# Delta-net layers in another column order, with one block substitution on VectorE

## The chip, the cores and the metric

The kernel runs on one core of one Trainium2 chip. The metric is the device time of one execution in microseconds. The kernel before takes 2232.32 us, the median of 3 runs (2231.94 to 2232.71). In the text PE is TensorE, DVE is VectorE, ACT is ScalarE, POOL is GpSimd and SP is SyncE, the engine that issues most transfers.

## The reference

Four layers work on 256 tokens of 1024 features. Each is a feed-forward half step, a token mixer and another feed-forward half step. The mixers of layers 0 and 3 are gated delta nets, that of layer 1 is a short convolution, that of layer 2 a sparse attention. Only the delta nets are touched by the change:

```python
def gdn_mixer(h, w_in, conv_w, A_log, dt_bias, out_norm, w_out):
    proj = h @ w_in                                   # queries, keys, values, gate: 4 x 1024; a, b: 2 x 8
    qkv, gate, a, b = jnp.split(proj, [...], axis=-1)
    qkv = jax.nn.silu(causal_depthwise_conv(qkv, conv_w))      # width 4
    q, k = l2norm(q), l2norm(k)                                # 8 heads of 128
    beta = jax.nn.sigmoid(b)
    g = -jnp.exp(A_log) * jax.nn.softplus(a + dt_bias)
    o = gated_delta_rule_chunked(q, k, v, g, beta)
    o = rmsnorm(o, out_norm) * jax.nn.silu(gate)
    return o @ w_out

# within a chunk: A = strictly lower part of (beta k) k^T times the decay;
# u and w are solutions with the unit triangular matrix (I + A); then a scan over the chunks:
v_new = u_c - w_c @ state
o = (q * decay) @ state + attn @ v_new
state = state * g_last + k_dec^T @ v_new
```

## The kernel before

All activations lie with features on partitions and the 256 tokens in the free dimension. Every product with weights is made three times in float32r, from two parts of the weights and two of the activations (`mm3`, L297 to L299). `Weights` streams the weights through 4 raw buffers. SP issues the loads (L90, L92) in the order of use, and a load waits until its buffer is free. ACT writes the high part (`hi`, L108, 128x1024) and DVE the rest (`lo`, L116); in the delta net, nine of the rests go to POOL instead (`tiles(..., nc.gpsimd, ...)`).

In the delta net (`gdn`) a `Dense` object emits the products one row tile at a time ("step": 6 matmuls of 256 columns), and after each step it lets every pending follow-up ("tail") emit its next piece (`pump`). So one order, fixed when the program is built, decides what stands behind what in the queue of each engine. `meet(condition)` emits steps until a tail has reached a state. When no products are left, steps emit only tails.

The columns come as 8 pairs (query, key) of a head, then 8 pairs (value, gate). `head_in` scales the product (L728), convolves (L695 on ACT, three L700 on DVE for each column tile) and applies silu through tanh (L703, L705). `head_mid` makes the transposes (L745), the decays (L748, L764 and the exponentials on ACT) and the products of keys with keys and queries (L753, L768). After 4 heads `lanes` starts for that half. It scales the matrices (L806), writes their 32x32 diagonal blocks to DRAM (L811, tile `db`), reads them back so that a partition holds a part of one block (L823, M in tile `gi`), inverts all 32 blocks by 31 steps of a multiplication and an addition on POOL (L830, L832, tile `g_inv`), writes the inverses to DRAM (L836, `di`) and reads them into their places on the diagonal (L840). `merges` then joins blocks of 32 to 64 and 128 (it begins with the transposes L852, then L870, L883, L887), `scan` runs the recurrence over two blocks of 128 tokens (L905 to L925) and `finish` norms, gates and splits the output (L937 to L956). This is done for heads 0 to 3 and then for heads 4 to 7; `wait(n)` lets a tail skip n steps. The output product (`add_rows_steps`) fills the second half's chain. The next norm begins with its sums of squares (L280).

The transfers of `lanes` go through SP's queue, between the loads of weights. The source of L823 is written out by hand; its leading dimension has 4 copies with stride 0:

```python
bass.AP(tensor=flat.tensor, offset=flat.offset, ap=[[0, 4], [1024, 32], [1, 1024]])
```

Of the kernel before, what the change touches and what calls it, by code (L numbers as in the profile page):

```python
# [28 lines left out]
class Weights:  # L29
    """Streams weights from DRAM in the order of use and splits them into two float32r parts whose  # L30
    sum is the float32 weight. A piece is what a run of products takes, in two halves."""
# [68 lines left out]
    def hi(self):  # L100
        """Writes the next half piece's part that float32r holds, once there is room for it."""
# [9 lines left out]
    def lo(self, engine=None):  # L111
        """Writes what remains of it."""
# [7 lines left out]
    def ahead(self, i, engine=None):  # L120
        """Every piece up to i has been split, as far as there is room."""
# [17 lines left out]
    def part(self, i, k):  # L139
        """Row tile k of piece i in its two parts."""  # L140
# [5 lines left out]
def kernel(ctx, tc, plan, a, out):  # L146
# [21 lines left out]
    def add_pairs(w):  # L168
        """Columns of the left half and the same of the right half."""
# [22 lines left out]
    def add_wide(w, c):  # L192
        """512 columns, each piece a half of the rows."""
# [40 lines left out]
    def busy(times):  # L234
        """The tensor engine's clock is at its full rate only after a few microseconds of products."""
# [12 lines left out]
    class Normed:  # L248
        """x * norm weight in two float32r parts, and the sums of squares on their way to the
        reciprocal root, which is applied behind the products."""  # L250
# [25 lines left out]
    def norm_sums(n):  # L276
        """The reciprocal roots, tokens on partitions."""
# [7 lines left out]
    def norm_rows(n):  # L285
        """The same for all partitions: a token to a column."""
# [17 lines left out]
    def rest(steps):  # L304
        """What a stream of steps returns at its end."""
# [6 lines left out]
    def output(k):  # L312
        """Two feature tiles of the result, tokens on partitions."""
# [9 lines left out]
    def add_rows_steps(pieces, inputs, ktiles, scale, next_col, engine=None):  # L323
        """x += scale * (inputs @ weights), the weights' rows in `pieces`; the next norm's start."""
# [44 lines left out]
    def first_cols(j, acc, ks, n):  # L369
        """The first products: those with the smaller parts of the weights behind the others."""  # L370
# [10 lines left out]
    def two_cols(j, acc, ks, n):  # L381
        """Two column tiles, which the piece keeps side by side in each row tile."""
# [15 lines left out]
    def two_first(pieces, n):  # L398
        """The first two pieces behind a norm."""
# [109 lines left out]
    def gdn_masks():  # L509
# [11 lines left out]
        def before(n, name):  # L521
            """The column's block of 2**n follows the row's in the same block of 2**(n + 1)."""
# [9 lines left out]
        G.half = const.tile([128, 8], F32, name="half")  # L532
        nc.vector.memset(G.half, 0.5)
        G.m1, p = before(5, "gm1")
        i32 = t2("i32", (8, 32), I32)
        nc.gpsimd.iota(i32, pattern=[[-4, 8], [1, 32]], base=0, channel_multiplier=0)
        G.eye32 = const.tile([128, 8, 32], F32, name="eye32")
        nc.vector.tensor_copy(G.eye32, i32)
        nc.vector.tensor_scalar(G.eye32, G.eye32, p[:, :1], None, op0=OP.is_equal)
        G.m2, _ = before(6, "gm2")  # L540
# [9 lines left out]
    def gdn_loads(g, i):  # L550
        """Everything small that the mixer needs, loaded during what comes before it."""
# [8 lines left out]
        on = small("onorm", (1,))  # L560
        nc.gpsimd.dma_start(on, a["gdn_out_norm"][i].rearrange("(p o) -> p o", o=1))
# [11 lines left out]
        g.on = small("onhalf", (1,))  # L573
        nc.vector.tensor_scalar(g.on, on, 0.5, None, op0=OP.mult)

    def gdn_decays(g, n):
        """The token gates: step sizes and cumulated log decays, tokens on partitions."""
# [25 lines left out]
        # log(1 + e) = 2 artanh(e / (2 + e)), the argument at most 1/3  # L603
# [23 lines left out]
    def converted(k, engine=None, other=None):  # L627
        """The conversions that go with a step of eight."""
# [7 lines left out]
    def tiles(j, n, engine=None, other=None):  # L636
        """Two column tiles, features on partitions."""
# [10 lines left out]
    class Dense:  # L648
        """Products by row tiles, and what is done with each, as a stream which is emitted in steps
        between those of a chain."""  # L650
# [28 lines left out]
        def products(self):  # L679
            """The rest of the products; tails may remain."""  # L680
# [11 lines left out]
    def conv_silu(t, taps, tiles, o):  # L692
# [3 lines left out]
        yield from wait(2)  # L696
# [5 lines left out]
        yield from wait(4)  # L702
        nc.scalar.activation(t, o, AF.Tanh, scale=0.5)  # L703
        yield from wait(2)
        nc.vector.scalar_tensor_tensor(o, t, 1.0, o, op0=OP.add, op1=OP.mult)  # L705
# [4 lines left out]
    def gdn(pieces, n, next_col, g):  # L710
        qk, vg, outs = pieces
        ss = small("ss", (2, 4, 2, 2))
        cq = small("gcq", (2, 4, 2))
        QK, H = {}, []
        for half in range(2):
            # by half of the heads: products of keys, queries in decays; two inverses; values, recurrence
            h = Gdn()
            h.ready, h.values = False, 0
            h.ga = b8(F32, "ga", (4, 2, 2, 128))
            k = b8(F32, "gk", (4, 4, 128))  # L720
            h.kE, h.kd, h.qd, h.g0 = (k[:, q] for q in range(4))
# [10 lines left out]
        def head_in(h, acc):  # L732
            t = yield from scaled(acc)
            o = l2("g_qk")
            yield from conv_silu(t, g.taps, (h, 8 + h), o)
            yield from wait(5)
            QK[h] = o

        def head_mid(h):
            x, f = QK[h], H[h // 4]  # L740
            e = h % 4
            pk = mid().rearrange("p (t s c) -> p t s c", t=2, s=2)
            for t in range(2):
                for s in range(2):
                    nc.tensor.transpose(pk[:, t, s], x[:, s, t * 128:(t + 1) * 128], ident)  # L745
            pg = mid()[:, :256].rearrange("p (t c) -> p t c", t=2)
            for t in range(2):
                nc.tensor.matmul(pg[:, t], g.g[:, t, h:h + 1].to_broadcast([128, 128]), G.tri,  # L748
                                 start=t == 0, stop=False, skip_group_check=True)
            pa = mid().rearrange("p (t s c) -> p t s c", t=2, s=2)  # L750
            for t in range(2):
                c = slice(t * 128, (t + 1) * 128)
# [240 lines left out]
        for _ in outputs(0, "mid"):  # L993
            dense.fill(2)
            if H[1].ready:
                next(other, None)
# [613 lines left out]
```

## Time and profile before

| what | value |
|---|---|
| median of 3 runs | 2232.32 us |
| profiled execution, span from first to last instruction | 2231.7 us |
| PE busy | 2149.7 us, 96% |
| DVE busy | 1427.9 us, 64% |
| ACT busy | 1067.2 us, 48% |
| POOL busy | 493.2 us, 22% |
| delta net of layer 0, from 203.4 us to the next norm's sums | 209.7 us, PE busy 184.0 |
| delta net of layer 3, from 1836.0 us to the next norm's sums | 207.5 us, PE busy 181.9 |

The busy shares are averages over stages with different limits, so the table sets the two delta nets apart. The time around the span is 0.6 us.

### The profile page before, as it was taken

How to read it: one execution, taken by the hardware profiler on the slowest of the kernel's cores; microseconds unless marked ns; L12 is line 12 of the kernel's file. 1: busy time of each engine (PE TensorE's matmuls, PEld its weight loads, DVE VectorE, ACT ScalarE, POOL GpSimd, SP SyncE). 2: the span in 40 equal slices, each digit the busy share in tenths (PEclk: the TensorE clock that was granted, in tenths of full speed). 3: DMA queues.
4: the chain of work that ended last, by engine and by line, in shares of the span. 5: the costliest groups of instructions: out<-in, count | busy, mean ns of one | idle time of the engine just before them, and what ended most of it. 6: DMA issues, size and time to landing. Idle time of an engine off the chain costs nothing.

```text
span 2231.7 us, 42671 instructions
## 1 busy us (share of the span) xinstructions
PE 2149.7 (96%) x17615; PEld 2105.6 (94%) x17615; DVE 1427.9 (64%) x2199; ACT 1067.2 (48%) x1830; POOL 493.2 (22%) x619
## 2 busy tenths in 40 slices
PE   8999879999999999999999988899999998979999
PEld 8999879999999999999999877699999998979999
DVE  7755975665566476664765577675566558956653
ACT  5444654544454354543544544454445445625542
POOL 2211473121022020220220233222002103741210
PEclk9999999999999999999999998999999999989999
DMA  7555253555465555655655432155546553524652
GB/s 247 191 190 166 87 135 105 166 189 189 160 199 190 185 174 166 212 189 182 187 190 198 161 123 71 44 188 187 192 150 211 190 170 114 138 86 130 204 196 76
DMA packets 285475, 364.33 MB, mean 163 GB/s; under 512 B 22640, under 2 KB 250096, under 8 KB 285280
## 3 DMA queue, kind: packets, MB, share of 16 engines
q1 hardware_dynamic: 284288, 360.26, 49.6%
q8 instruction: 138, 2.26, 0.4%
q0 software_dynamic: 944, 1.33, 0.3%
q14 instruction: 57, 0.47, 0.1%
q10 hardware_dynamic: 48, 0.02, 0.0%
HBM read 358.94 MB, written 2.10 MB: 162 GB/s over the span
## 4 chain that ended last, share of the span: by engine, by line
PE 82%; DVE 8%; POOL 5%; issue 2%; ACT 2%; DMA 1%; SPq 0%; POOLq 0%; ACTq 0%; DVEq 0%
PE acc L297 16%; PE acc L299 16%; PE acc L298 16%; PE mid L297 9%; PE mid L298 9%; PE mid L299 9%; DVE g_qk L700 2%; POOL g_inv L832 2%; POOL g_inv L830 2%; DMA gi<-db 1%; PE acc L1473 1%; PE mid L1193 1%; DVE wlo L116 1%; PE acc L1111 0%; PE acc L1113 0%
## 5 line engine op out<-in xcount | busy, mean ns | idle before, releaser
L297 PE MATMUL acc<-xhi,whi 128*128 128x256 f32 x3544 | 1006.6, 284 | 0.0
L299 PE MATMUL acc<-xhi,wlo 128*128 128x256 f32 x3544 | 996.7, 281 | 0.5 <-DVE wlo L116 0.5
L298 PE MATMUL acc<-xlo,whi 128*128 128x256 f32 x3544 | 996.4, 281 | 0.0
L116 DVE TENSOR_TENSOR wlo<-raw,whi 128x1024 fp32r<-128x1024 f32 x634 | 774.1, 1228 | 256.4 <-ACT whi L108 256.3
L108 ACT ACTIVATE whi<-raw 128x1024 fp32r<-128x1024 f32 x668 | 696.6, 1052 | 341.2 <-PE mid L298 279.8
L297 PEld LDWEIGHTS acc<-xhi,whi 128*128 128x128 f32 x3544 | 671.0, 189 | 8.3 <-issue 7.2
L298 PEld LDWEIGHTS acc<-xlo,whi 128*128 128x128 f32 x3544 | 670.8, 189 | 0.7
L299 PEld LDWEIGHTS acc<-xhi,wlo 128*128 128x128 f32 x3544 | 670.3, 189 | 0.7 <-DVE wlo L116 0.7
L297 PE MATMUL mid<-hhi,whi 128*128 128x256 f32 x1408 | 395.0, 281 | 0.0
L299 PE MATMUL mid<-hhi,wlo 128*128 128x256 f32 x1408 | 394.8, 280 | 0.0
L298 PE MATMUL mid<-hlo,whi 128*128 128x256 f32 x1408 | 394.8, 280 | 0.0
L428 POOL TENSOR_TENSOR t_h<-t_gate,rb 128x256 f32<-128x256 f32 x176 | 196.5, 1116 | 743.9 <-ACT t_gate L424 741.0
L298 PEld LDWEIGHTS mid<-hlo,whi 128*128 128x128 f32 x1408 | 265.3, 188 | 0.0
L299 PEld LDWEIGHTS mid<-hhi,wlo 128*128 128x128 f32 x1408 | 265.2, 188 | 0.0
L297 PEld LDWEIGHTS mid<-hhi,whi 128*128 128x128 f32 x1408 | 265.2, 188 | 0.0
L424 ACT ACTIVATE t_gate<-t_gate 128x256 f32<-128x256 f32 x176 | 73.6, 418 | 313.1 <-DVE t_gate L423 313.1
L423 DVE TENSOR_TENSOR t_gate<-acc,rb 128x256 f32<-128x256 f32 x176 | 74.3, 422 | 191.6 <-PE acc L299 191.6
L430 DVE TENSOR_TENSOR t_h<-acc,t_h 128x256 f32<-128x256 f32 x176 | 74.7, 424 | 127.6 <-POOL t_h L428 127.6
L435 ACT ACTIVATE hhi<-t_h 128x256 fp32r<-128x256 f32 x176 | 73.6, 418 | 150.0 <-DVE t_h L430 150.0
L116 POOL TENSOR_TENSOR wlo<-raw,whi 128x1024 fp32r<-128x1024 f32 x34 | 83.3, 2458 | 228.5 <-ACT whi L108 164.1
L283 POOL TENSOR_TENSOR rcol<-rcol,neghalf 128x2 f32<-128x2 f32 x12 | 8.5, 704 | 457.5 <-DVE rcol L282 457.5
L437 DVE TENSOR_TENSOR hlo<-t_h,hhi 128x256 fp32r<-128x256 f32 x176 | 73.7, 419 | 7.7 <-ACT hhi L435 7.7
(430 smaller groups left out, 2059.2 us busy)
## 6 DMA issues: line engine op xcount, KB each, us to landing
raw<-in_ffn_w_gate_up_dram SPq DMA_DIRECT2D x350, 512.0 KB, 4.9
raw<-in_ffn_w_down_dram SPq DMA_DIRECT2D x88, 1024.0 KB, 4.8
raw<-in_gdn_w_in_dram SPq DMA_DIRECT2D x64, 512.0 KB, 5.3
raw<-in_nsa_w_in_dram SPq DMA_DIRECT2D x10, 1024.0 KB, 4.9
raw<-in_gdn_w_out_dram SPq DMA_DIRECT2D x8, 1024.0 KB, 9.2
raw<-in_sc_w_in_dram SPq DMA_DIRECT2D x16, 512.0 KB, 4.5
raw<-in_sc_w_in_dram SPq DMA_DIRECT2D x4, 1024.0 KB, 6.7
raw<-in_sc_w_out_dram SPq DMA_DIRECT2D x4, 1024.0 KB, 5.5
```

The lines of the kernel that those rows point to most:

```text
L108: self.nc.scalar.activation(self.parts[g][0], raw, AF.Copy)
L116: (engine or self.nc.vector).tensor_sub(self.parts[g][1], self.half(g), self.parts[g][0])
L297: nc.tensor.matmul(o, w[0], x[0], start=first, stop=False, skip_group_check=True)
L298: nc.tensor.matmul(o, w[0], x[1], start=False, stop=False, skip_group_check=True)
L299: nc.tensor.matmul(o, w[1], x[0], start=False, stop=last, skip_group_check=True)
L423: nc.vector.tensor_mul(t, acc[:, 0], n.rb)
L424: nc.scalar.activation(s, t, AF.Silu)
L428: nc.gpsimd.tensor_mul(sr, s, n.rb)
L430: nc.vector.tensor_mul(h, acc[:, 1], sr)
L435: nc.scalar.activation(hi, h, AF.Copy)
L437: nc.vector.tensor_sub(lo, h, hi)
L700: nc.vector.scalar_tensor_tensor(o[:, s, j:], t[:, s, :S - j], taps[:, c:c + 1], o[:, s, j:], op0=OP.mult, op1=OP.add)
```

## The change

1. The weights' columns come in another order: keys of heads 0 to 3, values of heads 0 to 3, the same of heads 4 to 7, then the gates, then the queries. A product of keys, values or queries now covers two heads of one kind. All rests of weights (L116) are on DVE.
2. The gates are computed with tokens on partitions by `wide` (matmuls of 512 columns) and go through one silu each on ACT (L876), straight from PSUM. `finish` multiplies by them ahead of the transposes.
3. Values and queries use the silu of ACT (L856, L839). Keys keep the tanh.
4. `lanes` runs once for all 8 heads: 64 blocks of 32x32, a partition holds every second row of one, and the 31 steps are on DVE (L919, L923, L925). Its transfers are issued by ACT.
5. `merges` of both halves run side by side, then the two scans, offset by two stages. The output product starts behind most of them.

The core of the diff (the rest is the follow-ups' rearrangement into `keys_in`, `queries_in`, `values_in`, and comments):

```diff
-            steps.append((add_pairs(w[:, :2 * D]), add_pairs(w[:, 2 * D:4 * D]), add_rows(a["gdn_w_out"][i], D)))
+            kv = [add_cols(w, d + c, 512) for c in (0, 512) for d in (D, 2 * D)]
+            steps.append((kv, [add_wide(w, 3 * D + c) for c in (0, 512)], add_cols(w, 0, D),
+                          add_rows(a["gdn_w_out"][i], D)))
...
+        def gates_in(q, accs):
...
+                nc.scalar.activation(h.gates[t], accs[t].rearrange("p (e c) -> p e c", e=4), AF.Silu,
+                                     scale=n.r[:, t:t + 1])
...
-                nc.sync.dma_start(db[b].rearrange("h e c -> e h c"), h.B[r, :, r])
+                    nc.scalar.dma_start(db[b, 8 * q:8 * q + 8].rearrange("m e c -> e m c"), h.B[r, :, r])
...
-            nc.sync.dma_start(M.rearrange("p x c -> p (x c)"),
-                              bass.AP(tensor=flat.tensor, offset=flat.offset, ap=[[0, 4], [1024, 32], [1, 1024]]))
-            yield from wait(10)
+            nc.scalar.dma_start(M.rearrange("p x c -> p (x c)"),
+                                bass.AP(tensor=flat.tensor, offset=flat.offset, ap=[[0, 2], [1024, 64], [1, 1024]]))
+            yield from wait(LM)
...
             for k in range(31):
-                e, c = k // 4 + 1, 31 - k
+                e, c = k // 2 + 1, 31 - k
...
-                nc.gpsimd.tensor_mul(t, M[:, k:k + 1, k + 1:].to_broadcast([128, e, c]),
+                nc.vector.tensor_mul(t, M[:, k:k + 1, k + 1:].to_broadcast([128, e, c]),
                                      V[:, :e, k:k + 1].to_broadcast([128, e, c]))
-                nc.gpsimd.tensor_add(V[:, :e, k + 1:], V[:, :e, k + 1:], t)
...
+                nc.vector.tensor_add(V[:, :e, k + 1:], V[:, :e, k + 1:], t)
...
-                nc.sync.dma_start(di.rearrange("b h (i r) c -> (b h) r i c", r=4)[:, r], V[32 * r:32 * r + 32])
+                nc.scalar.dma_start(di.rearrange("b m (i r) c -> (b m) r i c", r=2)[:, r], V[64 * r:64 * r + 64])
...
-                nc.sync.dma_start(h.iv[r, :, r], di[b].rearrange("h e c -> e h c"))
+                nc.scalar.dma_start(iv[r, :, r], di[b].rearrange("m e c -> e m c"))
...
-        dense = Dense([(tiles(qk[h], n, nc.gpsimd if h > 0 else None, nc.gpsimd if h < 3 else None), lambda acc, h=h: head_in(h, acc[0])) for h in range(8)]
-                      + [(tiles(vg[m], n), lambda acc, m=m: vg_in(m, acc[0])) for m in range(8)])
+        dense = Dense([(tiles(kv[2 * q + x][e], n), lambda acc, p=2 * q + e, f=f: f(p, acc[0]))
+                       for q in range(2) for x, f in enumerate((keys_in, values_in)) for e in range(2)]
+                      + [(wide(gs[q], n), lambda accs, q=q: gates_in(q, accs)) for q in range(2)]
+                      + [(tiles(qs[p], n), lambda acc, p=p: queries_in(p, acc[0])) for p in range(4)])
...
+        dense.meet(lambda: "inverses" in done)
+        both = [merges(q, "mid") for q in range(2)]
+        for _ in both[0]:
+            next(both[1], None)
+            dense.fill(F1)
```

Where the transfers of the blocks stand. Before, SP's queue in layer 0 holds them between loads of weights:

```order
L90 DMA raw<-in_gdn_w_in_dram 128x4x256 x24
L811 DMA db<-ga 32x8x32 x4
L823 DMA gi<-db 128x1x1024
L90 DMA raw<-in_gdn_w_in_dram 128x4x256 x8
L811 DMA db<-ga 32x8x32 x4
L823 DMA gi<-db 128x1x1024
L92 DMA raw<-in_gdn_w_out_dram 128x2x1024 x2
L836 DMA di<-g_inv 256x1x32 x4
L840 DMA gi<-di 32x8x32 x4
```

After, ACT's queue holds them between its own work (here the second half's blocks, `db`, and the one load of M into `givt`):

```order
L108 ACTIVATE whi<-raw 128x1024 x2
L900 DMA db<-ga 32x8x32 x4
L826 ACTIVATE gk<-gk,ekd 128x128
L827 ACTIVATE gk<-gk,egc 128x128
L826 ACTIVATE gk<-gk,ekd 128x128
L827 ACTIVATE gk<-gk,egc 128x128
L868 ACTIVATE gv<-mid,gsv 128x128 x8
L911 DMA givt<-db 128x1x1024
L856 ACTIVATE g_vc<-g_vc 128x512
```

The load of M moved from SP's queue, where the blocks' writes stand directly ahead of it, into ACT's, where twelve small operations stand between.

Where the substitution stands. Before, POOL's queue in layer 0 has it almost to itself (`gk` is one product of queries and decays):

```order
L832 TENSOR_TENSOR g_inv<-g_inv 128x29
L830 TENSOR_TENSOR g_inv<-gi,g_inv 128x28
L832 TENSOR_TENSOR g_inv<-g_inv 128x28
L830 TENSOR_TENSOR g_inv<-gi,g_inv 128x54
L832 TENSOR_TENSOR g_inv<-g_inv 128x2x27
L762 TENSOR_TENSOR gk<-g_qk,g_dec 128x128
L830 TENSOR_TENSOR g_inv<-gi,g_inv 128x52
```

After, it is in DVE's queue, with the rests of the weights (`wlo`) between its steps:

```order
L116 TENSOR_TENSOR wlo<-raw,whi 128x1024 x4
L919 SCALAR_TENSOR_TENSOR givt<-givt 128x31
L919 SCALAR_TENSOR_TENSOR givt<-givt 128x30
L923 TENSOR_TENSOR givt<-givt 128x58
L925 TENSOR_TENSOR givt<-givt 128x2x29
L923 TENSOR_TENSOR givt<-givt 128x56
L925 TENSOR_TENSOR givt<-givt 128x2x28
```

The substitution moved from POOL to DVE; 4 rests of weights stand ahead of it, and 6 more and one L747 stand between its 60 operations.

## Rows read from the trace of the kernel before

**Rows 1.** The page's first part: busy time, share of the span, instructions.
```profile
span 2231.7 us, 42671 instructions
PE 2149.7 (96%) x17615; PEld 2105.6 (94%) x17615; DVE 1427.9 (64%) x2199; ACT 1067.2 (48%) x1830; POOL 493.2 (22%) x619
```

**Rows 2.** Windows, delta nets: length, busy PE, PEld, DVE, ACT, POOL, clock, DMA.
```profile
203.40:413.10 209.70, 184.04 (x1508) 178.65 (x1506) 158.95 (x261) 112.01 (x285) 93.57 (x156) 0.96 0.38 114
1836.00:2043.50 207.50, 181.86 (x1474) 176.52 (x1474) 155.33 (x253) 108.10 (x276) 93.37 (x156) 0.95 0.38 111
```

**Rows 3.** Windows, stretches of layer 0's delta net.
```profile
203.40:335.20 131.80, 108.74 (x869) 104.96 (x867) 111.66 (x175) 75.44 (x200) 75.65 (x113) 0.95 0.41 116
...
230.00:270.00 40.00, 32.95 (x247) 31.60 (x247) 37.30 (x49) 25.03 (x79) 17.90 (x11) 0.96 0.35 106
...
320.00:335.20 15.20, 2.44 (x22) 2.21 (x20) 5.14 (x8) 2.71 (x4) 12.30 (x39) 0.65 0.12 20
335.20:340.00 4.80, 4.80 (x30) 4.80 (x31) 0.77 (x2) 2.12 (x6) 3.86 (x13) 0.68 1.01 385
340.00:413.10 73.10, 70.50 (x612) 68.89 (x611) 46.51 (x85) 34.45 (x80) 14.06 (x32) 1.00 0.30 94
```

**Rows 4.** Waits of PE, 190 to 420 us: total, times, longest.
```profile
PE mid L852 <- DMA gi<-di: 12.8, 1, 12.8
PE mid L745 <- DVE g_qk L705: 4.1, 2, 3.4
PE mid L764 <- ACT g_dec L756: 4.0, 4, 2.3
```

**Rows 5.** Timeline of SP, POOL and PE: start, length, instruction, idle before.
```profile
274.39 0.65 SPq L823 DMA_DIRECT2D gi<-db  x1
...
284.92 0.39 POOL L830 TENSOR_TENSOR g_inv<-gi,g_inv 128x31 f32<-128x31 f32 x1 [5.84 <-DMA gi<-db]
...
327.35 0.21 POOL L832 TENSOR_TENSOR g_inv<-g_inv 128x8 f32<-128x8 f32 x1
...
327.58 2.60 SPq L836 DMA_DIRECT2D di<-g_inv  x4
...
335.17 1.97 PE L852 MATMUL mid<-ident,gi 128*128 128x128 f32 x8 [12.76 <-DMA gi<-di]
```

**Rows 6.** Windows while L823 alone moves data: length, clock, DMA share, GB/s.
```profile
274.00:276.00 2.00, 1.00 0.04 14
276.00:278.00 2.00, 1.00 0.25 80
```

**Rows 7.** Groups by form, DVE in the delta net: busy, mean ns.
```profile
L728 DVE TENSOR_TENSOR g_t<-acc,rb 128x512 f32<-128x512 f32 x16 | 10.9, 682 | 13.9 <-PE acc L299 13.8
L806 DVE TENSOR_TENSOR ga<-ga,gnD 128x1024 f32<-128x1024 f32 x2 | 2.4, 1224 | 0.1
```

**Rows 8.** Timeline and one group: DVE beside POOL's rests of weights.
```profile
223.13 2.95 DVE L700 SCALAR_TENSOR_TENSOR g_qk<-g_t,gtaps,g_qk 128x255 f32<-128x255 f32 x6
...
227.12 1.23 DVE L611 SCALAR_TENSOR_TENSOR gq<-gq,gs 128x16 f32<-128x16 f32 x6
...
228.47 7.04 DVE L700 SCALAR_TENSOR_TENSOR g_qk<-g_t,gtaps,g_qk 128x255 f32<-128x255 f32 x6
...
229.61 5.11 POOL L116 TENSOR_TENSOR wlo<-raw,whi 128x1024 fp32r<-128x1024 f32 x2
...
L116 POOL TENSOR_TENSOR wlo<-raw,whi 128x1024 fp32r<-128x1024 f32 x9 | 22.4, 2499 | 73.2 <-ACT whi L108 73.1
```

**Rows 9.** Timeline of DVE and ACT, and L811's issues (ns, min/median/max).
```profile
312.13 2.36 DVE L116 TENSOR_TENSOR wlo<-raw,whi 128x1024 fp32r<-128x1024 f32 x2
...
317.76 0.59 ACT L784 ACTIVATE gv<-acc,gsv 128x128 f32<-128x128 f32 x2
...
L811 SPq DMA_DIRECT2D db<-ga x16: 327/448/1282, 271.3 to 1930.3; - x16
```

**Rows 10.** The chain that ended last: a piece of PE's small matmuls.
```profile
362.49 1.73 PE acc L870 x16
```

More of the change, by code (lines that the diff above doesn't have):

```diff
@@ L248 @@
     class Normed:
+        pass
     def norm_start():
@@ L690, in wait, with conv @@
             yield
-    def conv_silu(t, taps, tiles, o):
+    LD = 10
+    F1 = 2
+    F2 = 3
+    F3 = 3
+    F4 = 3
+    LK = 20
+    LQ = 4
+    LV = 12
+    LM = 7
+    LS = 8
+    LT = 5
+    LP = 2
+    LE = 0
+    LF = 5
+    C1 = 2
+    C2 = 6
+    C3 = 1
+    def conv(t, taps, tiles, o):
         for s, m in enumerate(tiles):
             nc.scalar.activation(o[:, s], t[:, s], AF.Copy, scale=taps[:, 72 + m:73 + m])
-        yield from wait(2)
+        yield from wait(C1)
         for s, m in enumerate(tiles):
@@ L710, in gdn @@
     def gdn(pieces, n, next_col, g):
-        qk, vg, outs = pieces
+        kv, gs, qs, outs = pieces
         ss = small("ss", (2, 4, 2, 2))
-        cq = small("gcq", (2, 4, 2))
-        QK, H = {}, []
+        cq, n2, sv = small("gcq", (2, 4, 2)), small("n2", (2, 4, 2)), small("gsv", (2, 8))
+        done, H = set(), []
+        iv, ivt = b8(F32, "giv", (16, 128)), b8(F32, "givt", (16, 128))
         for half in range(2):
             h = Gdn()
-            h.ready, h.values = False, 0
+            h.keys = h.roots = h.values = 0
             h.ga = b8(F32, "ga", (4, 2, 2, 128))
             k = b8(F32, "gk", (4, 4, 128))
-            h.kE, h.kd, h.qd, h.g0 = (k[:, q] for q in range(4))
+            h.k2 = k[:, :2]
+            h.kd, h.kE, h.qd = (k[:, q] for q in range(3))
+            h.iv, h.ivt = iv[:, 8 * half:8 * half + 8], ivt[:, 8 * half:8 * half + 8]
+            h.K, h.sv = [None, None], sv[:, half]
+            h.gates = [k[:, 3]]
             H.append(h)
@@ new lines, in queries_in @@
+        def queries_in(p, acc):
+            q, e = p // 2, 2 * (p % 2)
+            f = H[q]
+            t = yield from scaled(acc)
+            while "lanes" not in done:
+                yield
+            o = t2("g_q")
+            yield from conv(t, g.taps, (2 * p, 2 * p + 1), o)
+            while ("decays", 3) not in done:
+                yield
+            nc.scalar.activation(o, o, AF.Silu)
+            yield from wait(LQ)
+            pk = turned(o)
+            pa = products(f.K[p % 2], o)
+            nc.gpsimd.tensor_mul(f.qd[:, e:e + 2], o[:, :, 128:], f.qd[:, e:e + 2])
+            yield
+            squares(pk, q, e, 0)
+            nc.vector.tensor_mul(f.ga[:, e:e + 2, :, 0], pa, f.ga[:, e:e + 2, :, 0])
+            done.add(("queries", p))
@@ new lines, in values_in @@
+        def values_in(p, acc):
+            f, e = H[p // 2], 2 * (p % 2)
+            t = yield from scaled(acc)
+            o = t2("g_vc")
+            yield from conv(t, g.taps, (16 + 2 * p, 17 + 2 * p), o)
+            while ("decays", 3) not in done or f.roots < e + 2:
+                yield
+            nc.scalar.activation(o, o, AF.Silu)
+            yield from wait(LV)
+            pv = turned(o)
+            if not hasattr(f, "v"):
+                w = b8(F32, "gv", (16, 128))
+                f.v, f.S = w[:, :8], w[:, 8:12]
+                f.gates.append(w[:, 12:])
+            yield
+            for x in range(2):
+                for t in range(2):
+                    c = 2 * (e + x) + t
+                    nc.scalar.activation(f.v[:, c], pv[:, x, t], AF.Copy, scale=f.sv[:, c:c + 1])
+            f.values += 1
@@ L978, in during, with decay_steps @@
-        def during(chain, steps):
-            for _ in chain:
-                dense.fill(steps)
-        dense.meet(lambda: H[0].ready)
-        during(merges(0, "mid"), 2)
-        dense.meet(lambda: H[0].values == 4)
+        norm_rows(n)
+        def decay_steps():
+            yield from wait(2)
+            next(decays)
+            yield
+            next(decays)
+            done.add("steps")
+            yield from wait(LD)
+            next(decays)
+            for p in range(4):
+                yield from wait(LE)
+                for _ in decayed(p):
+                    yield from wait(LF)
```

285 lines of the change are left out of this document (140 added, 145 removed).

## The prediction

> **What bounds the kernel now.** I read the page's first part first. PE is busy 96% of the span [rows 1], so a change can only return the time in which PE stands still, and PE's work has to be found unchanged or not. The windows by stage show where PE stands still: in the two delta nets it is busy 184.0 of 209.7 us and 181.9 of 207.5 us [rows 2], so 25.7 + 25.6 us of the span's 82 us of idle PE lie here. The finer windows [rows 3] split the first of them. From 320.0 to 335.2 us PE works 2.4 of 15.2 us, and in the 4.8 us behind that its granted clock is 0.68, so it works at near half speed there. From 340 us on it works 70.5 of 73.1 us. The waits of PE [rows 4] name the cause: 12.8 us in one wait of L852 for the transfer gi<-di, the inverses, and some 8 us in small waits for the keys' and decays' preparation (4.1 and 4.0).
>
> The chain behind the long wait is in the timeline [rows 5]: the load of M is issued at 274.4, POOL begins the substitution at 284.9 and ends it at 327.6, and the inverses are through DRAM and usable at 335.2. So the chain has 10.5 us of load, 42.7 us of POOL and 7.6 us of two transfers. All that follows takes 413.1 - 335.2 = 77.9 us, with PE nearly full. The change attacks the middle piece. Whether it gains is decided by when the new inverses are ready, since PE has to wait for them again.
>
> **PE's own work.** The small matmuls are the same in number, the products of weights too; wide ones have half the instructions of double length. Counted in the queues, 42 more small PE instructions than before stand behind the point where the inverses are needed (query transposes and products), and 42 fewer ahead of it. At 1.73 us for 16 [rows 10] they are 4.6 us. PE's own work up to the inverses is then 108.7 [rows 3] - 4.6 = 104 us; with waits as small as those of the keys now (8 us) PE would be there at about 203.4 + 112 = 315 us. So PE waits if the inverses come later than 315, and the stage ends later than now if they come later than about 335 - 4.6 = 330.
>
> **DVE up to the blocks.** All nine rests of weights that POOL had in this stage come to DVE: 9 x 1.18 = 10.6 us [rows 9]. Against that, a rest on POOL slows DVE beside it: six convolution steps take 2.95 us alone and 7.04 us while POOL's L116 runs [rows 8]; POOL has 22.4 us of those. So this exchange costs DVE nothing on balance, and I use undisturbed durations. The first convolution starts at about 224 us as now (223.1 [rows 8]). From there to the second scaling (L896, as L806 now) DVE's queue holds 7 convolutions of a pair of tiles, 12 rests, 15 operations of 512 columns, 2 scalings and some 14 tiny ones: 7 x 2.95 [rows 8] + 12 x 1.18 [rows 9] + 15 x 0.68 + 2 x 1.22 [rows 7] + 14 x 0.18 = 50 us, so 274 us without any wait. In 230 to 270 us DVE is now busy 37.3 of 40 us [rows 3]; at that rate it would be 277.6. I take 276.
>
> **ACT ahead of M.** The load of M now stands in ACT's queue behind 4 issues of transfers of 0.45 us and 12 small operations of 0.30 us [rows 9]: 5.4 us. It leaves at 281 us; the ends are 277 and 284. Now it leaves SP at 274.4 [rows 5], for half of the heads. Behind these issues ACT holds the high parts of weights; they have slack until DVE is through.
>
> **The load of M.** This is the price on which the sign hangs. Now it takes 10.5 us from issue to POOL's start [rows 5]: some 1.4 us until data flow, then 512 KB at 80 GB/s = 6.5 us, then the landing. At that time the 16 DMA engines are busy 0.25 in the mean [rows 6], so four of them carry it, and four is the number of copies in the leading dimension of its source. The new source has two copies in that dimension and 64 rows under each. If two engines carry it, the stretch in the middle doubles: 10.5 + 6.5 = 17 us. It also shares those two engines with up to two loads of weights, 1 MB each, that SP issues beside it; now such loads stand behind it in the same queue. The ends are 10.5 and 23 us. I take 18, since the quarter share of [rows 6] is the nearest row, and it fits the number of copies.
>
> The Trainium skill, "DMA: Bandwidth & Descriptors", section "Rules for kernel authors", states that a leading zero-stride broadcast of c copies confines a transfer to at most c engines. The trace agrees for four copies, by the 0.25 of [rows 6]; no run here shows two. By that rule the sum is the forecast's; by the duration of the row alone, 10.5 us, it is the first rival's.
>
> **Substitution and way back.** DVE has 60 operations for 62 x 2 on POOL (both halves). A tiny dependent one takes 1.23 / 6 = 0.205 us for 16 columns [rows 8], one of 512 columns 0.682 [rows 7], so 0.19 + 0.00096 for each column. The 58 large ones have 5590 columns together: 58 x 0.19 + 5.4 = 16.4, with the first two 16.9 us. Between them stand 6 rests and one L747: 6 x 1.18 + 0.68 = 7.8. So the inverses leave DVE 24.7 us after M: 281 + 18 + 24.7 = 323.7. The way through DRAM takes 7.6 us now [rows 5]; there are 6 issues instead of 8, but each write has four times the pieces of 128 bytes. I take 8.5, with ends 7.6 and 10.5. The inverses are ready at 332.2 us, against 335.2 now.
>
> So 42.7 us of POOL became 24.7 us of DVE, 18 us less, and the rest of the chain eats nearly all of it: it begins 6.6 us later because all 8 heads' keys come first, the load takes 7.5 longer, the way back 0.9. PE, done at about 315, waits some 17 us, as the 12.8 and 8 now. Before that it stands still too, since the first queries' rests stand behind the first steps of the substitution in DVE's queue; this is inside the same wait and costs nothing by itself.
>
> **Behind the inverses.** 77.9 us now, the loss of clock after the wait [rows 3] included, plus 4.6 us of small matmuls, plus 1.5 us (ends 0 and 5) because the two scans run one beside the other with no products of weights to fill them: 84.0. The stage ends at 332.2 + 84.0 = 416.2 instead of 413.1: 3.1 us later. The gates' silu, the changed `finish` and the single table load lie on ACT and DVE, which are 47% and 64% busy behind 340 us [rows 3]; nothing of them is on the path.
>
> **Sum.** Layer 3 has the same stage [rows 2]. 2 x 3.1 = 6.2 us. The profiled span is 2231.7, the median of the runs 0.6 above it: 2232.3 + 6.2 = **2238.5 us**.
>
> **Rivals.** First, M takes 10.5 us as now: the inverses come 7.5 us earlier than in the forecast, each stage ends 4.4 us sooner than now, 2238.5 - 15.0 = 2223.5. For it: the amount of data is the same and the copies may be spread otherwise. Against it: the 0.25 of [rows 6]. This is the one on the other side; it decides from a load of less than about 15 us, at which the stages end as now. By the rule of the skill it does not happen.
>
> Second, two engines carry M but DVE and ACT lose nothing on the way, and it leaves at 277: 4 us for each stage, 2230.5, which is no change that can be told. For it: POOL no longer disturbs DVE. Against it: 7% of idle DVE in the same stretch now [rows 3], from an alternation of ACT and DVE that the change keeps.
>
> Third, everything goes well: load of 10.5, issue at 277, way back 7.6, no wait in the scans. 7.5 + 4 + 0.9 + 1.5 = 13.9 us for each stage against the forecast, 2238.5 - 27.8 = 2210.7. PE's own arrival at 315 allows little more than that.
>
> Fourth, slower still: M shares its two engines with both loads of weights (23 us), and the scans wait 4 us instead of 1.5: 7.5 us for each stage, 2253.5. A further loss would be the granted clock, if PE goes through the whole stretch of waits at the 0.68 of [rows 3].
>
> That the change doesn't do what it says I leave out: the queues show that it does.
>
> **How the numbers follow.** Forecast 0.44, first rival 0.25, second 0.14, third 0.09, fourth 0.08. About 0.2% (4.5 us) can be told from no change here; the three runs lie 0.8 us apart. Faster: 0.25 + 0.09 = 0.34. Same: 0.14 and 0.04 of the forecast's own spread, which reaches below 2236.8. Slower: the rest, 0.48. Both signs hold much, so beside the range the forecast's own: 2233 to 2246. The range for 8 in 10 leaves out half of the third rival and most of the fourth: 2212 to 2252.
>
> **What would show it.** In the profile after: while M is on its way and weights are not, a DMA share near 0.12 and 40 GB/s (first rival: 0.25); a wait of DVE for givt<-db of over 8 us (second rival: M issued before 279); the 60 substitution operations within about 25 us; a wait of PE L946 for giv<-di, or for the queries' rests and it together, of some 17 us in each layer; POOL without L116 there, and six convolution steps never above 3.5 us. The prediction is wrong if PE has no long wait ahead of L946, if the chain to the inverses is under 325 us on the clock of layer 0, or if PE's instructions behind L946 take much more than 84 us.

## The result, and the profile after

| | before | after |
|---|---|---|
| median of the runs | 2232.52 us (4 runs, 2231.94 to 2233.1) | 2244.95 us (4 runs, 2243.7 to 2246.16) |
| profiled execution, span | 2231.7 us | 2244.4 us |

After takes 1.0056 of before's time, 95% interval 1.0042 to 1.007: slower, inside the range, and 6.45 us above the forecast. The page's first part, as in [rows 1], shows POOL 151 us less busy and PE standing still for 88.5 us instead of 82:

```profile
span 2244.4 us, 42086 instructions
PE 2155.9 (96%) x17487; PEld 2108.5 (94%) x17487; DVE 1415.5 (63%) x2282; ACT 1071.4 (48%) x1814; POOL 342.2 (15%) x344
```

The chain that the prediction added up stands in three timelines of layer 0 (start, length, instruction, idle before it). ACT issues the load of M and later the way back; DVE waits for M and goes through the substitution; PE waits for the inverses:

```profile
279.13 1.13 ACTq L911 DMA_DIRECT2D givt<-db  x1
279.37 1.65 ACT L868 ACTIVATE gv<-mid,gsv 128x128 f32<-128x128 f32 x6
...
321.37 1.28 ACTq L930 DMA_DIRECT2D di<-givt  x2
328.22 1.93 ACTq L934 DMA_DIRECT2D giv<-di  x4
```

```profile
274.56 1.22 DVE L896 TENSOR_TENSOR ga<-ga,gnD 128x1024 f32<-128x1024 f32 x1
...
282.51 2.36 DVE L116 TENSOR_TENSOR wlo<-raw,whi 128x1024 fp32r<-128x1024 f32 x2 [0.74 <-ACT whi L108]
297.23 0.53 DVE L919 SCALAR_TENSOR_TENSOR givt<-givt 128x31 f32<-128x31 f32 x2 [12.35 <-DMA givt<-db]
...
321.15 0.19 DVE L925 TENSOR_TENSOR givt<-givt 128x16 f32<-128x16 f32 x1
```

```profile
333.74 3.65 PE L946 MATMUL mid<-ident,giv 128*128 128x128 f32 x16 [12.94 <-DMA giv<-di]
```

The waits of PE in the same layer, beside [rows 4] (in all, times, longest). The long one is as long as before; a wait for rests that DVE could not write while it stood at L919 is new:

```profile
PE mid L946 <- DMA giv<-di: 12.9, 1, 12.9
PE acc L301 <- DVE wlo L116: 8.8, 2, 7.7
PE mid L788 <- ACT gk L785: 4.3, 1, 4.3
```

The windows by stage show a second thing. In [rows 2] layer 0's stage ended at 413.1 us; it now ends at 417.2, 4.1 us later. Layer 3's takes 2.8 us more (from the last product of the feed-forward step ahead of it to the next norm's sums: 1833.0 to 2043.4 before, 1842.7 to 2055.9 after). That is 6.9 of the 12.7 us between the spans. The other 5.8 lie in stages that the change does not touch. Three of them, before (length, then busy PE with its count) and after, PE full and its clock at 1.00 in all:

```profile
882.90:1069.70 186.80, 186.80 (x1593) 186.75 (x1592) 111.64 (x151) 88.98 (x122) 25.39 (x23) 1.00 0.57 187
1069.70:1257.30 187.60, 187.60 (x1566) 186.02 (x1564) 117.85 (x182) 89.74 (x125) 33.90 (x68) 1.00 0.58 189
1652.40:1833.00 180.60, 180.60 (x1534) 180.55 (x1533) 107.25 (x146) 82.65 (x114) 28.16 (x28) 1.00 0.58 190
```

```profile
887.10:1076.00 188.90, 188.90 (x1593) 188.84 (x1592) 111.64 (x151) 88.97 (x122) 25.34 (x23) 1.00 0.57 184
1076.00:1265.10 189.10, 189.10 (x1565) 187.58 (x1564) 117.76 (x182) 89.69 (x125) 33.86 (x68) 1.00 0.58 187
1660.70:1842.70 182.00, 182.00 (x1534) 181.94 (x1533) 107.20 (x145) 82.65 (x114) 28.12 (x28) 1.00 0.58 190
```

The same number of matmuls takes 2.1, 1.5 and 1.4 us longer (0.8 more are spread over the rest).

### The profile page after: what moved, and what is told of

Same layout as the page of the kernel before. It is cut to its first block, busy times and chain, and to the rows that moved or that the text cites. A ratio compares the mean times of both kernels' runs of the same rounds, so it can differ in the third digit from the quotient of the medians.

```text
span 2244.4 us, 42086 instructions
## 1 busy us (share of the span) xinstructions
PE 2155.9 (96%) x17487; PEld 2108.5 (94%) x17487; DVE 1415.5 (63%) x2282; ACT 1071.4 (48%) x1814; POOL 342.2 (15%) x344
## 3 DMA queue, kind: packets, MB, share of 16 engines
q0 software_dynamic: 944, 1.33, 0.3%
## 4 chain that ended last, share of the span: by engine, by line
PE 87%; DVE 6%; DMA 3%; ACT 3%; issue 1%; POOL 1%; ACTq 0%; SPq 0%; DVEq 0%; POOLq 0%
PE acc L299 17%; PE acc L301 17%; PE acc L300 17%; PE mid L299 9%; PE mid L300 9%; PE mid L301 9%; DMA givt<-db 2%; PE acc L1560 1%; DVE wlo L116 1%; PE mid L1280 1%; PE mid L964 1%; DMA di<-givt 1%; PE mid L977 0%; PE acc L1198 0%; DVE g_k L716 0%
## 5 line engine op out<-in xcount | busy, mean ns | idle before, releaser
L301 PE MATMUL acc<-xhi,wlo 128*128 128x256 f32 x3416 | 966.3, 283 | 17.9 <-DVE wlo L116 17.9
L299 PE MATMUL acc<-xhi,whi 128*128 128x256 f32 x3416 | 972.8, 285 | 0.0
L300 PE MATMUL acc<-xlo,whi 128*128 128x256 f32 x3416 | 965.6, 283 | 0.0
L116 DVE TENSOR_TENSOR wlo<-raw,whi 128x1024 fp32r<-128x1024 f32 x652 | 791.7, 1222 | 268.8 <-ACT whi L108 268.8
L301 PEld LDWEIGHTS acc<-xhi,wlo 128*128 128x128 f32 x3416 | 647.5, 190 | 18.8 <-DVE wlo L116 18.7
L299 PEld LDWEIGHTS acc<-xhi,whi 128*128 128x128 f32 x3416 | 647.8, 190 | 0.8
L300 PEld LDWEIGHTS acc<-xlo,whi 128*128 128x128 f32 x3416 | 647.7, 190 | 0.4
L262 ACT ACTIVATE xhi<-x,norms 128x256 fp32r<-128x256 f32 x96 | 43.2, 499 | 27.8 <-DVE x L342 21.3
```

The source lines that it names most:

```text
L116: (engine or self.nc.vector).tensor_sub(self.parts[g][1], self.half(g), self.parts[g][0])
L262: nc.scalar.activation(n.hi[:, kk], x[:, kk], AF.Copy, scale=norms[:, col + kk:col + kk + 1])
L299: nc.tensor.matmul(o, w[0], x[0], start=first, stop=False, skip_group_check=True)
L300: nc.tensor.matmul(o, w[0], x[1], start=False, stop=False, skip_group_check=True)
L301: nc.tensor.matmul(o, w[1], x[0], start=False, stop=last, skip_group_check=True)
```

## The experiments

Each is an edit of the kernel after, or of before where its name says so. The medians of before beside them were 2231.7, 2232.8, 2233.2 and 2232.9 us.

### The load of M on all engines: e1_m16, e2_before_m16

```diff
-                                bass.AP(tensor=flat.tensor, offset=flat.offset, ap=[[0, 2], [1024, 64], [1, 1024]]))
+            for r in range(2):
+                nc.scalar.dma_start(M[64 * r:64 * r + 64].rearrange("p x c -> p (x c)"), flat)
```

> After, with M loaded by two transfers of 64 partitions without a stride of 0, so that all engines can carry them. Theory: two engines are the reason for the 18.0 us of the load (50 GB/s, share 0.13). Then M lands 5 to 8 us after its issue, DVE goes on at about 285 us instead of 297.2 and its wait of 12.4 us goes; the inverses are ready 10 to 12 us earlier (322 to 324 instead of 333.7), PE's waits fall by 8 to 12 us in each layer, and the time is 2221 to 2229. Rival: the load is slow for another reason (the pieces of db just written, ACT's queue): then it stays at 18 us and the time at 2245.

Measured: 2220.77 us, 0.9946 of before (0.9931 to 0.9961). In after, while M alone moved data, two engines' share was busy (a window, as in [rows 6] with the busy times of the engines ahead of the clock):

```profile
281.40:282.80 1.40, 1.40 (x8) 1.13 (x7) 0.66 (x2) 1.40 (x3) 0.00 (x0) 1.00 0.13 53
```

0.13 is half of the share in [rows 6], at 53 GB/s. The Trainium skill, "DMA: Bandwidth & Descriptors", section "Rules for kernel authors", as cited in the prediction, agrees with this second value too. M was not alone for long. At its end, from 293 to 297 us, the share is still 0.13, but M (q10, ACT's queue) has only 7.1% of it and the weights (q1, SP's queue) have the rest (packets, megabytes, share):

```profile
q10 hardware_dynamic: 30, 0.11, 7.1%
q1 hardware_dynamic: 45, 0.09, 5.7%
```

So two loads of weights shared M's two engines. By its packets in the trace M moved data from 281.3 to 296.7 us, 15.4 us; at 53 GB/s its 512 KB alone would be 9.9 us (an estimate from the window above). In e1_m16 M is through when the loads of weights begin to move data, at 283 us: each of the two transfers lands some 4 us after its issue, DVE does not wait, and begins as soon as its rests are done:

```profile
285.27 0.53 DVE L919 SCALAR_TENSOR_TENSOR givt<-givt 128x31 f32<-128x31 f32 x2
```

So the chain is 12 us shorter in each layer, and the time 24 us: the stride of 0 alone decided the sign. The edit takes away both what two engines cost and what sharing them cost; no run parts the two. What PE still waits for there is the inverses, 11.7 us, and no rests.

> The kernel before, with M loaded by four transfers of 32 partitions without a stride of 0. Theory: four engines cost before 5 of its 10.5 us in each half, and the first half's stand on the path: POOL starts at 280 to 281 instead of 284.9, PE's wait ahead of L852 falls from 12.8 to 8 to 9, and the time is 2223 to 2226. Rival: the extra issues on SP and the loads of weights behind them eat it: 2230 to 2234.

Four transfers in place of four copies in the kernel before gave 2229.76 us, 0.9985 (0.9975 to 0.9994): 2 to 3 us where I expected 7 to 8, at the edge of the rival's range. POOL started at 278.75 instead of 284.92, as the theory had it, and the first wait fell to 8.0 us, but a new one of 2.7 stands at the second half's inverses:

```profile
PE mid L852 <- DMA gi<-di: 8.0, 1, 8.0
...
PE acc L852 <- DMA gi<-di: 2.7, 1, 2.7
```

POOL runs both halves one after the other, so a part of the 6 us is given back there; where the rest goes, or whether the extra issues of the rival have a share in it, these rows don't show.

### The way back: e3_back, e6_hold, e11_hold_m2

```diff
-            di = dram.tile([4, 16, 32, 32], F32, name="di", bufs=2)
+            di = dram.tile([2, 64, 16, 32], F32, name="di", bufs=2)
...
+            nc.scalar.dma_start(di.rearrange("r m i c -> (r m) (i c)"), V.rearrange("p i c -> p (i c)"))
...
+                for r in range(2):
+                    nc.scalar.dma_start(iv[32 * b + r:32 * b + 32:2, :, 32 * b:32 * b + 32],
+                                        di[r, 16 * b:16 * b + 16].rearrange("m i c -> i m c"))
```

> After, with the inverses written to DRAM as 128 rows of 2 KB instead of 2048 pieces of 128 bytes; the reads stay in pieces of 128 bytes, in 8 issues instead of 4. Theory: the way back takes 12.8 us instead of the 8.5 predicted because two loads of 1 MB from SP's queue run at the same time and each small piece waits its turn behind a large one (ACT's queue moved 1023 pieces in the us before them and 39 to 96 in the us beside them). Then di lands in 3 us instead of 6.2, the extra issues cost 2, and the inverses come 1 to 2 us earlier: 2241 to 2243. Rival: it is latency of two transfers and not the number of pieces; then 4 more issues make it 2 us later in each layer, 2248 to 2250.

Measured: 2242.35 us, 1.0051 (1.0032 to 1.0069). The interval holds after's 1.0056, so it tells the theories apart by its trace only: the reads are issued at 323.1 instead of 328.2 us, but eight issues of 0.63 us and the same loads beside the reads give it back, and PE starts at 332.8 instead of 333.7.

The next kernel takes the loads away from the way back. W is the stream of weights; while held it issues none:

```diff
-        while self.loaded < min(self.freed + self.LOADS, len(self.srcs)):
+        while not self.held and self.loaded < min(self.freed + self.LOADS, len(self.srcs)):
...
             yield from wait(LM)
+            W.held = True
...
-                nc.scalar.dma_start(di.rearrange("b m (i r) c -> (b m) r i c", r=2)[:, r], V[64 * r:64 * r + 64])
+                nc.sync.dma_start(di.rearrange("b m (i r) c -> (b m) r i c", r=2)[:, r], V[64 * r:64 * r + 64])
...
-                nc.scalar.dma_start(iv[r, :, r], di[b].rearrange("m e c -> e m c"))
+                nc.sync.dma_start(iv[r, :, r], di[b].rearrange("m e c -> e m c"))
+            W.held = False
+            W.load()
```

> e1_m16, with the way back (di, giv) issued by SP, and the loads of w_out held in SP's queue behind it, as before had it. In e1_m16 DVE ends the substitution at 309.3, the inverses are ready at 322.0, and PE waits 11.7 us for them and for nothing else. Theory: the 12.8 us of the way back are its small pieces standing beside 1 MB loads; without those it takes 7.5 to 9 as in before, PE's wait falls to 6.5 to 8, and the time to 2210 to 2213. Rival: it is two latencies (pieces alone, 4 times as many as before in a write): then it stays at 12 to 13 us and 2221. A third way: the held loads come too late for the output product, and PE waits there instead.

Measured: 2213.04 us, 0.9913 (0.9896 to 0.9929), with e7_all below the fastest of all. SP's queue shows the way back ahead of the loads, and PE starts 7.8 us after its issue:

```profile
309.10 1.27 SPq L931 DMA_DIRECT2D di<-givt  x2
312.72 1.94 SPq L935 DMA_DIRECT2D giv<-di  x4
314.76 2.13 SPq L92 DMA_DIRECT2D raw<-in_gdn_w_out_dram  x4
```

```profile
316.88 1.51 PE L949 MATMUL mid<-ident,giv 128*128 128x128 f32 x6 [6.99 <-DMA giv<-di]
```

Why it was slow shows in the queues of after from 324 to 327 us (packets, megabytes, share): SP's loads (q1) and ACT's write (q10) move the same number of packets, 232 of 4 KB and 227 of 128 bytes, one for one:

```profile
q1 hardware_dynamic: 232, 0.95, 85.9%
q10 hardware_dynamic: 227, 0.03, 6.2%
```

So a small piece waits for a large one each time. No third way showed: the output product does not wait for its held loads.

> After, M still on two engines, with only the way back of e6_hold: di and giv issued by SP with the loads of w_out behind them. It takes the one term of the sum that was sized too small, 12.8 instead of 8.5 us, back to the 7.8 of e6_hold. Theory: the stage shrinks by those 5 us in each layer, 2244.9 - 10 = 2235. Rival: with M late the rests of the queries' weights (PE's wait of 8.8 us for L116) end last, and the gain is under 5 us: 2240 or more.

This kernel has e6_hold's edit without that of M. Measured: 2237.61 us, 1.0023 (1.0013 to 1.0032), 0.33% or 7.4 us under after: 3.7 of the 5 us of each layer, between theory and rival. The wait for the inverses falls to 8.2 us; that for the rests, which the late M causes, stays:

```profile
PE acc L301 <- DVE wlo L116: 8.6, 2, 7.7
PE mid L949 <- DMA giv<-di: 8.2, 1, 8.2
```

The rival's reason is not what shows: PE still waits for the inverses last. From the start of the stage PE goes on 4.2 us sooner than in after in layer 0 and 5.0 in layer 3, as the theory has it; 1.1 and 0.5 us of that are lost again behind the inverses, and why is open.

### The substitution on POOL, and the rests on POOL: e8_pool, e12_pool_rests

```diff
-                nc.vector.tensor_mul(t, M[:, k:k + 1, k + 1:].to_broadcast([128, e, c]),
+                nc.gpsimd.tensor_mul(t, M[:, k:k + 1, k + 1:].to_broadcast([128, e, c]),
...
-                nc.vector.tensor_add(V[:, :e, k + 1:], V[:, :e, k + 1:], t)
+                nc.gpsimd.tensor_add(V[:, :e, k + 1:], V[:, :e, k + 1:], t)
```

> After, with the substitution of the 64 matrices on POOL (62 operations of up to 136 columns) and all else as in after: it prices part 4 by itself. POOL took 0.6 to 0.7 us for each operation of about 60 columns in before with its gaps; for 90 columns in the mean I expect 0.75, so 46 us instead of the 23.7 that DVE takes. Theory: the chain from M to PE's L946 is the path, so the stage grows by what the chain grows, 18 to 22 us a layer, some of it given back since DVE's 10 rests no longer stand between the steps: 2275 to 2290. Rival: the chain is not the path (PE's own waits for rests are); then 2245 to 2260.

Measured: 2247.76 us, 1.0066 (1.0051 to 1.0081), 3 us above after and not 30 to 45. The time is the rival's, but not for its reason: the chain is the path, since PE waits for the inverses alone. My price was wrong. The 62 operations take 30.7 us (297.6 to 328.2), 0.42 us busy each and a gap, where I had 46. And DVE is free for the rests, so PE waits once instead of twice:

```profile
PE mid L942 <- DMA giv<-di: 24.9, 1, 24.9
```

After's two waits are 12.9 + 8.8 = 21.7 us. The loads of w_out are through by then, and the way back takes 7.5 us on ACT's own queue, which is a second case of the mechanism of e6_hold. So POOL costs 6.6 us more than DVE (30.7 against 24.1), the later way back gives 4.9 of them back (7.5 against 12.4), and the engine of the substitution, the change's main idea, is worth 1 to 2 us a layer here. What it is worth where the way back is kept from the loads, as in e6_hold, no run shows.

The 42.7 us of POOL in before look long beside these 30.7 for twice the matrices. These are the stretches of the substitution, first in before (heads 0 to 3 only), then here (all heads), with the busy times of PE, PEld, DVE, ACT and POOL:

```profile
284.90:327.60 42.70, 37.17 (x312) 36.51 (x310) 38.83 (x62) 25.61 (x65) 38.13 (x68) 0.97 0.49 138
```

```profile
297.60:328.20 30.60, 13.22 (x112) 13.02 (x110) 8.29 (x12) 3.87 (x5) 25.82 (x62) 0.79 0.26 95
```

DVE is busy 38.8 of 42.7 us in before and 8.3 of 30.6 here. In before 13 of the 62 operations take 1.1 to 1.4 us, here 3, and each of them runs beside an L116 or L806 of DVE, of 1.2 us each. That DVE is the reason is argued from these rows; no run changes it alone.

```diff
+        pool = [(nc.gpsimd if h > 0 else None, nc.gpsimd if h < 3 else None) for h in range(8)]
-        dense = Dense([(tiles(kv[2 * q + x][e], n), lambda acc, p=2 * q + e, f=f: f(p, acc[0]))
+        dense = Dense([(tiles(kv[2 * q + x][e], n, *pool[4 * q + 2 * x + e]), lambda acc, p=2 * q + e, f=f: f(p, acc[0]))
```

> After, with the rests of the weights shared between DVE and POOL as before had it: 10 of the first 16 pieces of keys and values on POOL. The prediction took this exchange at nothing on balance: DVE has 10 x 1.18 = 11.8 us less, but beside a rest on POOL six convolution steps took 7.04 us instead of 2.95. In after these steps take 2.95 us throughout and M is issued at 279.1 us. Theory: the load of M is issued between 277 and 281 again and the time is 2242 to 2248. Rival: what DVE is relieved of counts in full, M leaves 8 to 12 us earlier and the time is 2221 to 2229. Other rival: POOL's rests slow more than the convolutions, or PE waits for them; then M leaves later and the time is over 2250.

Measured: 2259.56 us, 1.0116 (1.0097 to 1.0135), 13 us above after: the other rival. M leaves at 287.0 instead of 279.1 us. Six convolution steps take 7.01 us beside two rests on POOL, as in [rows 8]:

```profile
230.40 7.01 DVE L716 SCALAR_TENSOR_TENSOR g_k<-g_t,gtaps,g_k 128x255 f32<-128x255 f32 x6 [0.58 <-ACT g_k L711]
```

```profile
231.79 4.83 POOL L116 TENSOR_TENSOR wlo<-raw,whi 128x1024 fp32r<-128x1024 f32 x2 [4.28 <-ACT whi L108]
```

and some 5 us beside one (four groups of 4.97 to 5.09), 2.1 above their 2.95. A rest on DVE costs it 1.22 us; a rest on POOL, which takes 2.4 us there, costs DVE 2.1. The Trainium skill, "SBUF — State Buffer", section "SBUF: two separate sides", says that a DVE operation with two SBUF inputs and a GpSimd operation that reads SBUF lock each other out for a whole instruction; these rows agree, with 4.1 us of delay for 4.83 us of POOL.

### PE's two paces: before_again, e4_pad, e7_all, e9_pad992, e10_before_pad

The stages with 5.8 us more differ in one thing. From the starts of PE's products in the traces: in an even stream of 256-column products one starts every 117.34 ns or every 118.67 ns, at full clock, and the pace holds until other matmuls come between. Counted in groups of 24, some 4900 of 13900 such products of before run at the quick pace; 4900 x 1.33 ns = 6.5 us. In after fewer than 300 do.

> The kernel before, unchanged, for a second profile. After's span is 12.7 us longer; by the marks of the norms the two delta nets account for 4.3 and 2.9 us, and 5.5 us lie in feed-forward stages that the change does not touch. There PE starts a product of 256 columns every 117.34 ns in four stretches of before (27 to 85, 887 to 1073, 1110 to 1297, 1715 to 1898 us) and every 118.67 ns everywhere in after; both at full granted clock. Theory: which of the two paces a stretch has is fixed by the program, so the fast stretches stand at the same places again and the span is within 1 us of 2231.7. Rival: the paces are chance of one execution; then the places differ and the time moves by several us.

Measured: 2232.44 us, 1.0003 (0.9994 to 1.0012); some 5400 quick products. From 784 us on the stretches are where they were; between 26 and 320 us most quick and slow ones have changed places. So both had a part: later in the program the places are the same in both executions, early in it they differ. (The span was 2235.8, since the attention layer between 1300 and 1470 us took some 4 us longer in that execution.)

```diff
-        G.odd = const.tile([128, 1], F32, name="oddlane")
+        G.odd = const.tile([128, 9], F32, name="oddlane")[:, :1]
```

> After, with one constant tile made 32 bytes larger for each partition and nothing else changed. The second profile of before has its products at 117.3 ns in nearly the same places as the first (5424 and 4944 of 13872 products in even streams), and after, and after with another M load, in 288 and 240 of some 14000: so the program decides it. In the built programs the feature tiles that PE streams (xhi, xlo, hhi, hlo) begin at multiples of 64 bytes in before and 32 bytes behind one in after, because the diff takes constants away. Theory: this offset holds PE to 118.7 ns. With 32 bytes more the offset goes; products run at 117.3 ns in at least as many places as in before, and the time is 5 to 8 us lower, 2237 to 2240. Rival: the order of the instructions decides the pace and not the place of the tiles; then 2243 to 2246.

Measured: 2242.37 us, 1.0041 (1.0026 to 1.0056); fewer than 300 quick products. The time lies between theory and rival and can't be told from after's 1.0056 (1.0042 to 1.007), and the pace is after's: the 32 bytes alone are not the cause. e7_all, with both edits, says the same:

> e6_hold with the 32 bytes of e4_pad. If both theories hold the gains add up: 5 to 8 us below e6_hold, 2203 to 2207. If only one holds, it is as that kernel against its base.

Measured: 2213.02 us, 0.9911 (0.9896 to 0.9926), beside e6_hold's 2213.04; fewer than 300 quick products.

> e6_hold with 992 bytes of unused constants, so that the tiles of the activations begin at the same bytes as in before; the 32 bytes of e4_pad changed nothing in the pace (264 fast products of 13896). Theory: the place of these tiles decides the pace after all, over more than 64 bytes; then some 5000 products run at 117.3 ns again and the time falls by 5 to 7 us, from 2213 to 2206 to 2208. Rival: the place has no part in it; fewer than 300 fast products and 2212 to 2214.

Measured: 2214.9 us, 0.9919 (0.9902 to 0.9935); fewer than 300 quick products. With the activations at the very bytes of before, the pace of before does not come back.

> The kernel before with 32 bytes of constants more, which moves its activations off the multiples of 64 bytes, as they lie in after. If the place decides the pace, the fast stretches (5000 to 5600 products in three profiles) go and the time rises by 5 to 7 us, to 2238. If not, they stay and it is 2231 to 2233.

Measured: 2236.53 us, 1.0019 (1.0009 to 1.0028), between the two; some 3500 quick products, in other places (the stretch at 940 us is gone). Windows of 60 us with PE full show it, at 480, 940 and 1160 us (length, busy PE with its count, clock, DMA share, GB/s; 514 products is quick, 508 slow), first before, then this kernel, then after:

```profile
480.00:540.00 60.00, 60.00 (x508) 1.00 0.56 192
940.00:1000.00 60.00, 60.00 (x514) 1.00 0.58 194
1160.00:1220.00 60.00, 60.00 (x514) 1.00 0.55 194
```

```profile
480.00:540.00 60.00, 60.00 (x508) 1.00 0.56 190
940.00:1000.00 60.00, 60.00 (x508) 1.00 0.57 194
1160.00:1220.00 60.00, 60.00 (x514) 1.00 0.56 198
```

```profile
480.00:540.00 60.00, 60.00 (x508) 1.00 0.57 194
940.00:1000.00 60.00, 60.00 (x508) 1.00 0.57 187
1160.00:1220.00 60.00, 60.00 (x508) 1.00 0.59 205
```

Neither place nor chance alone explains them. The four profiles of kernels with before's order have some 3500 to 5600 quick products, the ten of after and its variants fewer than 300, whatever the tiles' place. What in the program decides stays open.

## Why the prediction was right, and where it was off

Layer 0, step by step, each as the prediction named it:

| step | predicted | measured |
|---|---|---|
| second scaling on DVE ends | 276 us | 275.8 |
| M leaves | 281 | 279.1 |
| load of M | 18 us long | 18.1 |
| substitution with what stands between | 24.7 | 24.1 |
| way back | 8.5, ends 7.6 to 10.5 | 12.4 |
| inverses ready | 332.2 | 333.7 |
| behind the inverses | 84.0 | 83.5 |
| end of the stage, 413.1 before | 416.2 | 417.2 |

(The expectations above count the way back as 12.8, from 320.9 us, where the last operation but one of the substitution starts.)

- **The sign** hung on the load of M, as written. The quarter share of [rows 6] read as one engine for each copy gave 18 us, and 18.1 came. Two engines are shown; that the total is right to 0.1 us is luck. The prediction had 13 us of data at 40 GB/s and 1 us for sharing the engines with the weights. Measured, the data alone would be 9.9 us at 53 GB/s, and sharing made 15.4 of them; the rest, 2.7 us, is start and landing, where the prediction had 4. e1_m16 shows the other side of the sign. That its 2220.8 lies near the 2223.5 of the first rival is partly luck too: there DVE goes on 5.8 us after the first issue and not 10.5, which is worth some 9 us in both layers, and the way back and PE's pace cost about as much.
- **ACT ahead of M** took 3.3 us and not 5.4, since six of the twelve small operations counted ahead of the load run behind its issue in the trace (L868, 279.4 us). That makes up the 1.9 us by which M left earlier.
- **The way back is the term that was sized too small**: 12.4 instead of 8.5, outside its ends. The prediction had seen the danger for M (loads on another queue beside it) but not for the way back, where in before SP's one queue kept the loads behind the pieces. e6_hold gives 7.8 without the loads. Of its 3.9 us, 3.0 were made up elsewhere: M left 1.9 earlier, the substitution took 0.6 less and what stands behind the inverses 0.5 less. With the load's 0.1 that leaves the 1.0 us by which the stage ended later than forecast.
- **DVE and POOL.** The 50 us from undisturbed durations were right within 3 us (223.0 to 275.8). But "this exchange costs DVE nothing on balance" was wrong: e12_pool_rests shows that with the rests on POOL M leaves 8 us later. The sum didn't need that sentence, since it counted all rests on DVE. What "18 us less" for POOL's 42.7 claims for the change of engine is too much as well: with DVE mostly idle beside it POOL does both halves' work in 30.7 us (e8_pool), so the engine itself gave 6.6.
- **PE's wait** of some 17 us was 12.9 for the inverses and 8.8 for the rests, together 21.7, the latter "inside the same wait" as written: when M comes early both shrink (e1_m16).
- **Layer 3** costs 2.8 us instead of 3.1. Both delta nets are 6.9 us, 6.2 predicted.
- **What the sum didn't have**: 5.8 us in stages without any edit, from PE's pace. Without these the time would have been about 2239. The step "PE's own work" counted instructions and took their duration as given. Why the pace is another is open, so nearly half of the 12.7 us between the spans has a place (PE, at full clock) but no shown cause. The wide range has room for a term of this size that nobody had counted; the forecast's own 2233 to 2246 held the result by 1 us.
- **Two small readings.** 42 instructions at 1.73 us for 16 are 4.5 us, not 4.6. The clock of 0.68 in [rows 3] is a mean: PE ran at half clock, 0.50, to 338 us, and at 1.00 from 339.

## What to carry to other kernels

Before a transfer is moved to another queue, look at what shared its old one: in one queue large loads wait behind small pieces, from another they take turns with them, packet by packet. A load that reads the same data several times is written as several loads without a stride of 0, and the DMA share of a window in which it moves alone tells how many engines carry it. Before an operation is moved to another engine, price the chain to its end: here the transfers around it were worth 32 us, and the engine 6.6 us in each layer on its own step, but 3 us in the time, since the earlier end ran into the loads.

## What the runs showed that was not expected

- Two queues on the same engines took turns packet by packet whatever their size: 232 of 4 KB against 227 of 128 bytes in 3 us.
- A load on two engines took 15.4 us for what would be 9.9 alone, since loads of weights used the same two.
- Even streams of the same product ran at 117.34 or 118.67 ns each with the clock at 1.00; the pace changed only where other matmuls came between, and one program kept to mostly the same one.
- A group of six convolution steps went from 2.95 to 7.01 us beside two rests on POOL, and to about 5 beside one. The other way round, operations of POOL that take 0.2 to 0.5 us elsewhere took 1.1 to 1.4 beside a DVE operation of 1.2 us.
